# The last two whole-tile stores of a row-gradient kernel move from the SP queue to the ACT queue

## The chip, the core and the metric

The kernel runs on one core of a Trainium2 chip. The metric is the device time of one execution in microseconds (us). Five executions of the kernel before took 1249.83 to 1254.77 us, with a median of 1252.14 us. One further execution was recorded by the profiler; its own time is given with the profile below.

## The reference

The input `x` is a matrix of 8192 x 8192 float32 values, and the output has the same shape:

```python
def reference(x):
    return np.gradient(x, axis=1)
```

Along each row, every inner element is half the difference of its right and its left neighbour. The first element of a row is `x[1] - x[0]`, and the last one is `x[8191] - x[8190]`. Every value is read once and written once: 268.44 MB in and 268.44 MB out.

## The kernel before, in words

**Tiling.** The 8192 rows are cut into 32 sets (`nsets`) of 256 rows. A set lies in SBUF as one tile of 128 partitions, with `R = 2` whole rows of the matrix in each partition, so a set is 16384 float32 per partition (64 KB) and 8.39 MB in all. There are `NB = 3` tiles, called slots; set `i` uses slot `i % 3`. Each slot has 64 spare elements in front, so that the result can be written in place, shifted by those 64 elements.

**What happens to a set.** SP issues the load (line 72). GpSimd (POOL), in `put_aside` (line 84), takes the four end differences of each partition into a small tile `ends`. VectorE (DVE), in `work` (line 102), computes the half differences of the whole tile in place with one custom instruction. A small copy (line 116) puts the end values from `ends` into the result; it is done by ScalarE (ACT) for odd sets and by DVE for even ones (`placer`). Then the `storer` engine waits for that copy (line 117) and issues the store to HBM (line 118).

**The order of transfers.** There are two hardware DMA queues in use, one fed by SP and one by ACT. Each is served in the order in which its engine issued. SP's program is: loads 0, 1 and 2 at once; after that, one load per set. Before load `i` (from 3 on), SP waits at lines 68 and 69 for two things: that load `i - 1` has landed, and that the store which empties the slot, that of set `i - 3`, has landed. Below, this pair of waits is called the gate.

**The end of the program.** Sets 0 to 28 are followed by a further load, and their stores are issued by ACT. Set 31 is loaded as two halves, row 0 and row 1 of each partition (4.19 MB each, with 32 KB per partition), so that its work and its stores go row by row, all on DVE and SP. In the order of the program, SP does the following at the end:

1. load 30 (gate: load 29 and store 27);
2. the gate of load 31 (load 30 and store 28), then the two row loads of set 31;
3. the stores of sets 29 and 30 (`i + NB < nsets` is false for these two), each after a wait for its copy;
4. the stores of row 0 and row 1 of set 31, each after a wait for its copy;
5. the last waits for all stores (lines 140 and 142).

An engine's instructions run in order, so what stands behind a wait on SP is not issued before that wait is over.

Of the kernel before, what the change touches and what calls it, by code (L numbers as in the profile page):

```python
# [1 line left out]

# [4 lines left out]


@with_exitstack
def kernel(  # L10
    ctx: ExitStack,
    tc: tile.TileContext,
    x: bass.AP,
    out: bass.AP,
):

    nc = tc.nc
    P = nc.NUM_PARTITIONS
    n, m = x.shape
    R = 2
    NB = 3
    SH = 64  # L30
    W = R * m
    nsets = n // (P * R)
    f32 = x.dtype

    x_sets = x.rearrange("(s p t) m -> s p (t m)", p=P, t=R)
    out_sets = out.rearrange("(s p t) m -> s p (t m)", p=P, t=R)

    pool = ctx.enter_context(tc.tile_pool(name="pool", bufs=1))
    slots = [pool.tile([P, SH + W], f32, name=f"slot{k}", tag=f"slot{k}") for k in range(NB)]
    ends = pool.tile([P, nsets, R, 2], f32, name="ends", tag="ends")  # L40

    with tc.tile_critical():  # L42
        ld = [nc.alloc_semaphore(f"ld{k}") for k in range(NB)]
        st = [nc.alloc_semaphore(f"st{k}") for k in range(NB)]
        ld_rows = [nc.alloc_semaphore(f"ld_row{r}") for r in range(R)]
        st_rows = [nc.alloc_semaphore(f"st_row{r}") for r in range(R)]

        aside = [nc.alloc_semaphore("aside"), 0]
        halved = [nc.alloc_semaphore("halved"), 0]
        placed = {  # L50
            nc.vector: [nc.alloc_semaphore("placed_dve"), 0],
            nc.scalar: [nc.alloc_semaphore("placed_act"), 0],
        }

        def done(ins, counter):
            ins.then_inc(counter[0])
            counter[1] += 1
            return counter[0], counter[1]

        ld_n, st_n = [0] * NB, [0] * NB  # L60

        def load(i):
            k = i % NB
            if i < NB:
                parts = [(ld[k], 0, R)]
            else:

                nc.sync.wait_ge(ld[(i - 1) % NB], 16 * ld_n[(i - 1) % NB])
                nc.sync.wait_ge(st[k], 16 * st_n[k])  # L69
                parts = [(ld[k], 0, R)] if i < nsets - 1 else [(ld_rows[r], r, 1) for r in range(R)]  # L70
            for sem, r0, nr in parts:
                nc.sync.dma_start(
                    out=slots[k][:, SH + r0 * m : SH + (r0 + nr) * m],
                    in_=x_sets[i, :, r0 * m : (r0 + nr) * m],
                ).then_inc(sem, 16)
            ld_n[k] += 1

        def put_aside(i, r0, nr, sem, count):

            k = i % NB  # L80
            xin = slots[k][:, SH + r0 * m : SH + (r0 + nr) * m].rearrange("p (t m) -> p t m", m=m)
            nc.gpsimd.wait_ge(sem, count)
            return done(
                nc.gpsimd.tensor_sub(  # L84
                    out=ends[:, i, r0 : r0 + nr, :],
                    in0=xin[:, :, 1 : m : m - 2],
                    in1=xin[:, :, 0 : m - 1 : m - 2],
                ),
                aside,
            )  # L90

        def work(i, r0, nr, ready, placer, storer, sem):

            b = slots[i % NB]
            c0, c1 = r0 * m + 1, (r0 + nr) * m - 1
            mid = b[:, c0:c1]
            after = b[:, SH + c0 + 1 : SH + c1 + 1]
            before = b[:, SH + c0 - 1 : SH + c1 - 1]
            nc.vector.wait_ge(*ready)

            at = done(
                nc.vector._custom_dve(  # L102
                    dve_ops.TENSOR_TENSOR_REDUCE_SUB_MAX,
                    out=mid,
                    in0=after,
                    in1=before,
                    s0=0.0,
                    s1=0.5,
                ),
                halved,  # L110
            )
            res = b[:, r0 * m : (r0 + nr) * m].rearrange("p (t m) -> p t m", m=m)
            to, of = res[:, :, 0 : m : m - 1], ends[:, i, r0 : r0 + nr, :]
            placer.wait_ge(*at)
            copy = nc.scalar.copy if placer is nc.scalar else nc.vector.tensor_copy
            at = done(copy(out=to, in_=of), placed[placer])  # L116
            storer.wait_ge(*at)
            storer.dma_start(
                out=out_sets[i, :, r0 * m : (r0 + nr) * m],
                in_=b[:, r0 * m : (r0 + nr) * m],  # L120
            ).then_inc(sem, 16)

        for i in range(NB):
            load(i)
        for i in range(nsets):
            k = i % NB
            if i < nsets - 1:
                ready = put_aside(i, 0, R, ld[k], 16 * ld_n[k])
                placer = nc.scalar if i % 2 else nc.vector
                storer = nc.scalar if i + NB < nsets else nc.sync  # L130
                work(i, 0, R, ready, placer, storer, st[k])
                st_n[k] += 1
            else:
                for r in range(R):
                    ready = put_aside(i, r, 1, ld_rows[r], 16)
                    work(i, r, 1, ready, nc.vector, nc.sync, st_rows[r])
            if i + NB < nsets:
                load(i + NB)
        for r in range(R):
            nc.sync.wait_ge(st_rows[r], 16)  # L140
        for k in range(NB):
            nc.sync.wait_ge(st[k], 16 * st_n[k])


# [1 line left out]
_INS = ['x']  # L146
_OUTS = [((8192, 8192), 'float32')]


# [23 lines left out]
```

## Time and profile before

The profiled execution took 1253.39 us, and its span, from the first to the last instruction, is 1251.4 us; the remaining 2.0 us lie around the span.

| What | Value |
|---|---|
| median of five executions | 1252.14 us |
| profiled execution, its span | 1253.39 us, 1251.4 us |
| DVE busy | 554.2 us (44% of the span), 51 instructions |
| POOL busy | 15.1 us (1%) |
| ACT busy | 4.2 us |
| SP's DMA queue | 5328 packets, 293.60 MB, 54.7% of 16 engines |
| ACT's DMA queue | 4176 packets, 243.27 MB, 44.9% of 16 engines |
| mean transfer rate over the span | 429 GB/s |
| whole-tile DVE instruction (line 102) | 17.2 us |
| one-row DVE instruction (line 102) | 8.6 us |

How to read it: a DMA of 128 partitions is split over 16 DMA engines, and each engine takes 8 partitions. The page counts 9505 packets, of which 1056 are under 512 bytes. The 66 DMAs (33 loads, 33 stores) have 66 x 128 = 8448 data packets and 66 x 16 = 1056 small ones that count a semaphore up, which is 9504. So a data packet is one partition's contiguous run: 64 KB for a whole tile, 32 KB for a row of set 31. In the records of single DMA packets, which the trace also holds, a 64 KB packet takes 2.42 us on its engine and a 32 KB packet 1.21 us. Eight of the first are 19.3 us, which is what a whole tile costs the 16 engines.

### The profile page before, as it was taken

What the parts mean: (1) busy time and instruction counts of PE and PEld (TensorE: products, weight loads), DVE (VectorE), ACT (ScalarE), POOL (GpSimd) and SP (SyncE); (2) the same over time, 40 slices, a digit from 0 to 9 for tenths busy, and PEclk for the clock granted to TensorE, in tenths of its full rate; (3) what the DMA queues carried; (4) which work ended last, traced back from release to release, by engine and by line L of the source; (5) the groups of instructions that cost most, each with busy time, mean ns of one, the idle gap of its engine ahead of it and who ended that gap; (6) DMA issues with size and microseconds to landing.
All of it is one profiled execution on the core that took longest, in us unless ns stands there. A gap on an engine that the chain in (4) does not pass through costs nothing.

```text
span 1251.4 us, 254 instructions
## 1 busy us (share of the span) xinstructions
DVE 554.2 (44%) x51; ACT 4.2 (0%) x16; POOL 15.1 (1%) x37
## 2 busy tenths in 40 slices
DVE  2841552445533455433554335543355533555640
ACT  0000000000000000000000000000000000000000
POOL 0000000000000000000000000000000000000110
DMA  9999999999999999999999999999999999999998
GB/s 402 436 436 434 436 436 432 434 432 436 421 434 429 432 434 429 432 436 432 425 434 436 436 436 436 436 434 432 432 434 429 434 432 429 427 436 434 372 439 373
DMA packets 9505, 536.88 MB, mean 429 GB/s; under 512 B 1056, under 2 KB 1056, under 8 KB 1056
## 3 DMA queue, kind: packets, MB, share of 16 engines
q1 hardware_dynamic: 5328, 293.60, 54.7%
q10 hardware_dynamic: 4176, 243.27, 44.9%
q14 instruction: 1, 0.01, 0.0%
HBM read 268.44 MB, written 268.44 MB: 429 GB/s over the span
## 4 chain that ended last, share of the span: by engine, by line
DMA 92%; DVE 4%; issue 0%; POOL 0%; SPq 0%
DMA slot<-in_x_dram 89%; DVE slot L102 4%; DMA out_dram<-slot 3%; DVE slot L116 0%; POOL ends L84 0%; SPq L168 0%; SPq L69 0%; SPq L42 0%
## 5 line engine op out<-in xcount | busy, mean ns | idle before, releaser
L102 DVE CUSTOM_DVE_ANT_0 slot<-slot 128x16382 f32<-128x16382 f32 (+1 forms) x33 | 551.3, 16706 | 649.0 <-POOL ends L84 649.0
L84 POOL TENSOR_TENSOR ends<-slot 128x4 f32<-128x4 f32 (+1 forms) x33 | 14.9, 450 | 1179.5 <-DMA slot<-in_x_dram 1179.5
L116 ACT COPY slot<-ends 128x4 f32<-128x4 f32 x15 | 3.0, 197 | 1111.9 <-DVE slot L102 1111.9
L116 DVE COPY slot<-ends 128x4 f32<-128x4 f32 (+1 forms) x18 | 3.1, 172 | 0.6
L116 ACT ACT_TABLE_LOAD x1 | 1.3, 1283 | 41.1 <-DVE slot L116 41.1
L157 POOL MEMSET const-bfloat16-1.0<- 128x1 bf16 x1 | 0.1, 101 | 0.0
L157 POOL MEMSET const-uint8-127<- 128x1 uint8 x1 | 0.1, 101 | 0.0
L157 POOL MEMSET const-float32-0.0<- 128x1 f32 x1 | 0.1, 98 | 0.2 <-issue 0.2
L157 POOL MEMSET const-float32-1.0<- 128x1 f32 x1 | 0.1, 98 | 0.0
## 6 DMA issues: line engine op xcount, KB each, us to landing
slot<-in_x_dram SPq DMA_DIRECT2D x2, 4096.0 KB, 17.3
out_dram<-slot SPq DMA_DIRECT2D x2, 4096.0 KB, 45.3
slot<-in_x_dram SPq DMA_DIRECT2D x31, 38.6
out_dram<-slot ACTq DMA_DIRECT2D x29, 38.1
out_dram<-slot SPq DMA_DIRECT2D x2, 42.8
```

The source lines that it names most:

```text
L84: nc.gpsimd.tensor_sub(out=ends[:, i, r0 : r0 + nr, :], in0=xin[:, :, 1 : m : m - 2], in1=xin[:, :, 0 : m - 1 : m - 2],),
L102: nc.vector._custom_dve(dve_ops.TENSOR_TENSOR_REDUCE_SUB_MAX, out=mid, in0=after, in1=before, s0=0.0, s1=0.5,),
L116: at = done(copy(out=to, in_=of), placed[placer])
L157: nc = _bacc.Bacc("TRN2", target_bir_lowering=False, num_devices=1)
```

## The change

The choice of the engine that issues a whole-tile store is dropped; ACT issues them all. This concerns sets 29 and 30, whose stores were issued by SP. Set 29 is odd, so its copy is done by ACT as well; set 30 is even, so its copy is done by DVE. The two row stores of set 31 stay on SP, and so do all loads and all gates.

```diff
             if i < nsets - 1:
                 ready = put_aside(i, 0, R, ld[k], 16 * ld_n[k])
                 placer = nc.scalar if i % 2 else nc.vector
-                storer = nc.scalar if i + NB < nsets else nc.sync
-                work(i, 0, R, ready, placer, storer, st[k])
+                work(i, 0, R, ready, placer, nc.scalar, st[k])
                 st_n[k] += 1
```

## The prediction

> **What bounds the kernel now.** I read the page's engine rows first: DVE is busy for 44% of the span, POOL and ACT for about 1% together, so no compute engine is the bound. The chain of waits says the same by line:
>
> ```profile
> by line: DMA slot<-in_x_dram 88.6%; DVE slot L102 4.1%; DMA out_dram<-slot 3.3%; issue 0.1%; DVE slot L116 0.1%; POOL ends L84 0.0%; SPq L168 0.0%; SPq L69 0.0%; SPq L42 0.0%
> ```
>
> Transfers carry the span from end to end. So the question is whether the 16 DMA engines are ever without work. I cut the span into stretches (columns: stretch, length, DVE, ACT and POOL busy, clock, mean busy share of the DMA engines, GB/s):
>
> ```profile
> 46.00:1156.00 1110.00, 497.43 (x43) 2.76 (x14) 5.54 (x28) 1.00 1.00 433
> 1156.00:1172.00 16.00, 4.24 (x2) 0.20 (x1) 0.20 (x1) 1.00 0.74 307
> 1172.00:1250.00 78.00, 31.68 (x6) 0.00 (x0) 8.72 (x2) 1.00 0.98 417
> ```
>
> The reader is to see that the engines are full for 1110 us, and then there is one hole of 16 x (1 - 0.74) = 4.2 us, or by bytes 16 x (1 - 307/433) = 4.7 us. Both include packets cut at the stretch's ends. The records of single packets give it exactly: summed over the 16 engines and divided by 16, they idle 3.3 us between 1164.8 and 1170.3, and nowhere else between the first packet (2.0) and the last (1248.7 to 1249.2).
>
> The timeline of the end says why:
>
> ```profile
> 1139.49 29.80 SPq L72 DMA_DIRECT2D slot<-in_x_dram  x3
> 1157.03 0.20 ACT L116 COPY slot<-ends 128x4 f32<-128x4 f32 x1 [77.45 <-DVE slot L102]
> 1168.53 0.20 POOL L84 TENSOR_TENSOR ends<-slot 128x4 f32<-128x4 f32 x1 [28.79 <-DMA slot<-in_x_dram]
> 1169.34 34.80 SPq L118 DMA_DIRECT2D out_dram<-slot  x4
> ```
>
> Load 30 is issued at 1139.49 and has landed by 1168.46. Store 28 landed at 1156.4 (line 69's last wait ends there). From then on load 30 is the only transfer. Store 29 is ready at 1157.25, but it stands on SP behind the gate of load 31 and is issued only at 1169.34, 12.1 us late. When load 30 runs out, every queue is empty, until the row loads issued at 1168.5 bring their first packets at 1169.4 to 1170.3.
>
> **The change, part by part.** *What moves.* Two DMA issues of 0.34 us each go from SP to ACT, with their waits. ACT has nothing behind them: the copy of set 29 is its last work, and the wait for DVE's copy of set 30 holds up nobody. On SP only the row stores stood behind them. No load waits for stores 29 or 30. So the issues cost nothing themselves; what changes is when the packets enter the rings. The stores stay in the same set of bytes.
>
> *What it gains at most.* Before, an average engine's last packet ends at 1249.0. Count what it has left at 1160.9, the first packet boundary at which store 29 could appear: of load 30 two packets on 12 engines and three on 4 (2.25 on average), and 8 each for store 29, load 31, store 30 and the two row stores in 64 KB units, 34.25 in all. At 2.418 us each that is 82.8 us, to 1243.7. The difference of 5.3 us is the hole (3.3), the first row packets after it (1.9 instead of 1.2 us), and the last two row loads on each engine, which take 1.9 and 2.0 us instead of 1.2. With no idle anywhere, the slowest engine, about 1.5 us behind the mean (load 30's packets end between 1165.3 and 1167.8), ends at 1245.2; landing is seen 0.6 us later, 1245.8, where SP's last wait now ends at 1204.2 + 26.1 + 19.3 = 1249.6. The most to be had is 3.8 us.
>
> *What is late next.* Store 29 now runs beside load 30 and slows it: on a ring that both queues use, the records show the engines taking one packet of each in turn. Load 30's last two packets wait for a store packet each, so it ends near 1170.6 and lands at about 1171 (at 1175 on an engine with three left). The row loads are issued then; an engine in use takes 4 to 6 us to reach a new DMA (store 28: issued 1116.0, first packet 1119.3 to 1119.8; store 0: 40.67 and 46.9), so they join at about 1175, when half of store 29 is left.
>
> Now row loads of 32 KB packets compete with stores of 64 KB packets, which the trace before never shows: there the rows ran alone. Bounded from both sides: if the engines take turns by packet, the rows get one third of the bytes; if by bytes, half. [...]
>
> By packets: four store packets and four row packets alternate from 1175.4 to 1189.9. Set 30's work on DVE begins at 1171.3 and its store is issued at 1171 + 0.3 + 17.2 + 0.2 = 1188.7, joining at about 1194. Until then the rows run alone (3 to 4 packets). Then about 9 row packets face 8 of store 30, in turn. So when row 1 has landed, practically all of load 30, store 29, load 31 and store 30 is out: 26.25 packets of 2.418 us from 1160.9, 1224.4 on average, 1225.9 on the slowest engine, landed 1226.5.
>
> Behind that stands a chain that was covered before (row 1 had landed by 1191.6 and its store stood in a full queue):
>
> ```profile
> 1191.60 3.23 POOL L84 TENSOR_TENSOR ends<-slot 128x2 f32<-128x2 f32 x1 [5.56 <-DMA slot<-in_x_dram]
> 1194.89 8.68 DVE L102 CUSTOM_DVE_ANT_0 slot<-slot 128x8190 f32<-128x8190 f32 x1
> 1203.61 0.17 DVE L116 COPY slot<-ends 128x2 f32<-128x2 f32 x1
> ```
>
> POOL's 3.23 us is a wait for DVE; free, it takes 0.2. So row 1's store is issued 0.3 + 8.6 + 0.2 = 9.1 us after landing, at 1235.6. Meanwhile the only work is the row 0 store (ready at about 1207, queued behind row 1's load): 8 x 1.21 = 9.7 us from 1224.4 to 1234.1. The rings then run dry again. Row 1's first packets come 0.9 to 1.8 us after issue, as those of the rows did after 1168.5, at 1236.9; 9.7 us for eight, 0.5 for a slow first one, and 0.6 to landing end it at 1247.7.
>
> *The sum.* 1249.6 becomes 1247.7: 1.9 us gained of the 3.8. Span 1251.4 - 1.9 = 1249.5, the profiled execution 1253.39 - 1.9 = 1251.5. That execution lies 1.25 us above the median of the runs shown; the same 1.9 us off the median is **1250.2 us**.
>
> [...]
>
> **The rivals.**
>
> *The hole closes wholly.* If a row load gets its half by bytes, or if one or two of store 30's packets are still queued when row 1 lands (9 against 8 is narrow, and a packet is 2.4 us), row 1's chain is covered and the work alone sets the end: 3.8 us gained, 1248.3. For it: row 1 needs to land only 2 to 3 us earlier. [...]
>
> *Slower: small packets stretch beside large stores.* The last two row loads of each engine, just ahead of the first store packet, took 1.9 and 2.0 us instead of 1.2, so a row packet near a store can lose 0.7 to 0.8 us. Now all 16 row packets of an engine pass among store packets. At half that price each, 16 x 0.38 = 6 us are added ahead of row 1's landing, and the chain behind it shows all of it: 1250.2 + 6 = 1256.2. It overturns the gain from 0.12 us a packet, and is over 0.2% slower from 0.28. Against it: 64 KB loads and stores alternate at 2.42 us with no loss.
>
> *No change.* The later landing of load 30 and row 1 gives back everything: if row 1 lands 2 us later than worked out (one more engine with three packets, a slower join), the second dry spell is as costly as the first: 1252.1.
>
> **How the numbers follow.** 0.2% is 2.5 us, about what a measurement of this kernel can tell from no change. Half closed (1250.2, own range 1248.7 to 1251.7): 0.50. Wholly closed (1248.3): 0.25. Slower by stretched packets (1256.2): 0.16. No change (1252.1): 0.09. Faster by over 0.2% is below 1249.6: 0.3 of the first case, 0.85 of the second, little else: 0.37. Slower is 0.8 of the third, with a little of the last: 0.15. The rest, 0.48, is within. The range goes from 1247.4 (second case less the 1 us by which medians scatter) to 1253.4 (no change with the same scatter, the first step of the third case); about 0.15 is left out.
>
> **What would show it.** Store 29 issued on ACT at about 1157.3, and no dip in the DMA share around 1166: the first step. Row loads issued at 1171 to 1175 instead of 1168.5: the second. POOL's row 1 operation at about 1226 instead of 1191.6: arbitration by packets; at 1215 to 1219, by bytes. A dip in the DMA share between 1234 and 1237, and a chain that ends row 1, POOL, DVE, store: the second dry spell. Row packets of 1.6 us or more: the slower rival. I am wrong from the start if the dip near 1166 remains with store 29 issued early.

## The result, and the profile after

The changed kernel took 1249.49 us (median of 19 executions), the kernel before 1252.85 us (median of 37 on the same chips). The ratio is 0.9968, with a 95% interval of 0.9958 to 0.9977: 4.0 us faster (2.9 to 5.3). A few executions of several kernels, these two included, took 1322 to 1339 us; they are left out of every ratio here and below (the two medians alone differ by 3.4 us). The gain is more than the 0.2% that can be told from no change. The time lies inside the predicted range and 0.7 us below the predicted 1250.2. That nearness is partly luck: the prediction took its 1.9 us off a median of five executions, 1252.14, which lies 0.7 us under the median of 37. The gain itself is about twice the predicted one: what came is the first rival, "the hole closes wholly" (3.8 us). The chance given to "faster" was 0.37.

The profiled execution took 1250.89 us with a span of 1248.7 us, 2.5 us less than the profiled execution of before. The same three stretches as before (columns: stretch, length, DVE, ACT and POOL busy, clock, mean busy share of the DMA engines, GB/s):

```profile
46.00:1156.00 1110.00, 497.62 (x43) 2.77 (x14) 5.59 (x28) 1.00 1.00 433
1156.00:1172.00 16.00, 0.94 (x1) 0.20 (x1) 0.00 (x0) 1.00 1.02 442
1172.00:1250.00 78.00, 35.12 (x6) 0.00 (x0) 0.59 (x3) 1.00 0.91 393
```

The first row is unchanged, 433 GB/s. In the second, 0.74 has become 1.02 (a packet counts whole in the stretch in which it starts, which can carry a share over 1). The hole is gone: by the packet records no engine idles there. The third row is lower than before mainly because the transfers end earlier inside it.

Rows of the timeline of the end (a row that holds several DMA issues, x2 or x3, runs from the first issue to the end of the last):

```profile
1139.43 39.76 SPq L72 DMA_DIRECT2D slot<-in_x_dram  x3
1157.20 38.96 ACTq L118 DMA_DIRECT2D out_dram<-slot  x2
1178.13 0.20 POOL L84 TENSOR_TENSOR ends<-slot 128x4 f32<-128x4 f32 x1 [38.45 <-DMA slot<-in_x_dram]
1197.43 0.20 POOL L84 TENSOR_TENSOR ends<-slot 128x2 f32<-128x2 f32 x1 [19.10 <-DMA slot<-in_x_dram]
1206.58 26.97 SPq L118 DMA_DIRECT2D out_dram<-slot  x2
1224.06 0.20 POOL L84 TENSOR_TENSOR ends<-slot 128x2 f32<-128x2 f32 x1 [26.43 <-DMA slot<-in_x_dram]
```

Store 29 is issued by ACT at 1157.20 instead of 1169.34. Load 30 pays for that: POOL sees it land at 1178.13 instead of 1168.53, and the row loads are issued after that. Row 1 is seen by POOL at 1224.06 instead of 1191.60. Load 30, the rows of set 31 and DVE's work on them are all later, and the kernel is faster, because before the change the end waited for none of them: they had time to spare.

The end of the chain of waits (columns: start, length, what):

```profile
1178.46 45.53 DMA slot<-in_x_dram
1223.99 0.07 issue
1224.06 0.20 POOL ends L84
1224.26 0.02 issue
1224.29 8.70 DVE slot L102
1232.99 0.02 issue
1233.01 0.17 DVE slot L116
```

This is the chain that the prediction feared: row 1's load, POOL, DVE, copy, store. It is now the one that ended last, but it costs little. By the packet records the engines idle 0.4 us on average in front of row 1's store, between 1233.4 and 1234.2, against 3.3 us in the old hole. Below, such an idle time in front of row 1's store is called the dry spell.

### The profile page after: what moved, and what is told of

It is laid out like the page before. It is cut to its first block, busy times and chain, and to the rows that moved or that the text cites. A ratio compares the mean times of both kernels' runs of the same rounds, so it can differ in the third digit from the quotient of the medians.

```text
span 1248.7 us, 254 instructions
## 1 busy us (share of the span) xinstructions
DVE 554.4 (44%) x51; ACT 4.2 (0%) x16; POOL 6.8 (1%) x37
## 2 busy tenths in 40 slices
DMA packets 9504, 536.88 MB, mean 430 GB/s; under 512 B 1056, under 2 KB 1056, under 8 KB 1056
## 4 chain that ended last, share of the span: by engine, by line
DMA 96%; DVE 2%; issue 0%; POOL 0%; SPq 0%
DMA slot<-in_x_dram 93%; DMA out_dram<-slot 3%; DVE slot L102 2%; POOL ends L84 0%; DVE slot L116 0%; SPq L72 0%; SPq L167 0%; SPq L69 0%; SPq L42 0%
## 5 line engine op out<-in xcount | busy, mean ns | idle before, releaser
L84 POOL TENSOR_TENSOR ends<-slot 128x4 f32<-128x4 f32 (+1 forms) x33 | 6.6, 199 | 1217.2 <-DMA slot<-in_x_dram 1217.2
```

The lines of the kernel that those rows point to most:

```text
L84: nc.gpsimd.tensor_sub(out=ends[:, i, r0 : r0 + nr, :], in0=xin[:, :, 1 : m : m - 2], in1=xin[:, :, 0 : m - 1 : m - 2],),
```

## The experiments

Two explanations of the gain compete. **Theory A**: the gain is the filled hole. **Theory B**: the gain is that two queues share the last 80 us, where SP alone carried everything. Four kernels tell them apart; the diffs are against the kernel before unless another is named.

**Only store 29 on ACT**

```diff
-                storer = nc.scalar if i + NB < nsets else nc.sync
+                storer = nc.sync if i == nsets - 2 else nc.scalar
```

> Only store 29 goes to ACT; store 30 stays on SP behind the row loads. Theory A (the gain is the hole at 1165 to 1170, filled because store 29 no longer stands behind the gate): 3 to 5 us faster than before, as much as the full change; DMA share near 1.00 from 1156 to 1172; row 1 lands near 1204, since no ACT store competes with it, so no dry spell near 1233. Theory B (the gain is that two queues share the last 80 us, where SP alone carried everything): clearly less than the full change, 1 to 2 us.

Measured: 0.9973 (0.9962 to 0.9983), 3.4 us faster. The hole is filled:

```profile
1156.00:1172.00 16.00, 3.44 (x1) 0.20 (x1) 0.00 (x0) 1.00 1.03 446
```

Row 1 lands at 1211.1, later than expected since load 30 again landed only at 1178.5. After store 29 no store on ACT competes with the rows, and there is no dry spell. As A says, store 29 alone brings the gain, within the intervals.

**Only store 30 on ACT**

```diff
-                storer = nc.scalar if i + NB < nsets else nc.sync
+                storer = nc.sync if i == nsets - 3 else nc.scalar
```

> Only store 30 goes to ACT; store 29 stays on SP behind the gate of load 31. Theory A: the hole stays (share about 0.74 from 1156 to 1172), load 31 is issued near 1168.5, and the time is that of before within 1 us. Theory B: two queues are in use from about 1186 on, so most of the gain is there, 2 to 4 us faster.

Measured: 0.9992 (0.9982 to 1.0003), no difference. The stretch of the hole in this kernel:

```profile
1156.00:1172.00 16.00, 3.93 (x2) 0.20 (x1) 0.20 (x1) 1.00 0.78 322
1172.00:1250.00 78.00, 32.35 (x6) 0.00 (x0) 8.49 (x2) 1.00 0.99 422
```

The hole is there (0.78; 2.7 us by the packet records), and two queues from 1186.9 on bring nothing. B falls.

**All stores where they were, but load 31 does not wait for load 30** (it still waits for store 28; below, "no gate")

```diff
-                nc.sync.wait_ge(ld[(i - 1) % NB], 16 * ld_n[(i - 1) % NB])
+                if i < nsets - 1:
+                    nc.sync.wait_ge(ld[(i - 1) % NB], 16 * ld_n[(i - 1) % NB])
```

> All stores where they were before, but load 31 waits for store 28 alone and not for load 30, so the row loads are issued near 1156.5 behind load 30 on the same queue, and store 29 follows at about 1157.3. Theory A: no hole, 3 to 5 us faster than before, with ACT's queue empty for the last 90 us. Theory B: no gain, since SP alone carries everything from 1156 on.

Measured: 0.9965 (0.9954 to 0.9977), 4.4 us faster. The row loads stand behind load 30 on SP, and store 29 behind them:

```profile
1156.00:1172.00 16.00, 4.02 (x2) 0.20 (x1) 0.20 (x1) 1.00 0.94 406
```

The 0.94 is again a matter of which packets start inside the stretch: by the packet records no engine idles between 1110 us and the end. ACT's queue is empty for the last 90 us, and the gain is there all the same. It is the wait that cost, not the queue.

**Both stores on ACT, but ACT waits for load 30** (against the changed kernel)

```diff
             storer.wait_ge(*at)
+            if i == nsets - 3:
+                storer.wait_ge(ld[(nsets - 2) % NB], 16 * ld_n[(nsets - 2) % NB])
```

> Both stores on ACT as in the change, but ACT waits for load 30 to land before it issues store 29. Theory A: the hole is back, share about 0.74 from 1156 to 1172, and the time is that of before within 1 us. Theory B: two queues share the last 80 us, so the gain of the full change stays, 3 to 4 us.

Measured: 1.0099 (1.0086 to 1.0112), 12 us slower than before. Neither theory said that. The hole is back (2.3 us by the packet records), but most of the loss comes after it:

```profile
1172.00:1205.00 33.00, 15.67 (x2) 0.00 (x0) 0.00 (x0) 1.00 0.98 365
1205.00:1222.00 17.00, 8.86 (x2) 0.00 (x0) 0.20 (x1) 1.00 1.00 360
```

Engines busy all the time, at 360 GB/s instead of 433: the packets themselves are longer. From 1165 on, a 64 KB store packet on ACT's queue takes 2.92 us on average instead of 2.42, and a row load packet 1.41 instead of 1.21. In the changed kernel the same kinds of packets also pass each other in turn, at 2.42 and 1.21. With 16 store and 16 row packets on each engine, that is 16 x 0.50 + 16 x 0.20 = 11.2 us. Row 1 lands at 1243.4, and in front of its store the engines run dry for 3.3 us. This is the slower rival of the prediction, in a kernel where it was not looked for. Two readings: **theory C**, small packets beside large ones are slow in themselves, or **theory D**, the load and the store must start together, as they do here (store 29 is issued at 1170.06, the rows at 1169.99 and 1170.37), so that each engine moves the same place of both in turn.

**The changed kernel without the gate of load 31** (the edit of the third kernel above)

> The change, and load 31 no longer waits for load 30: its rows stand behind load 30 on SP and meet the second half of store 29 and all of store 30 on ACT, with the rows two or three partitions away from the stores' packets. Theory C (32 KB row packets and 64 KB store packets in turn are slow in themselves, which made the run with ACT's wait 13 us slower): row packets or the store packets beside them stretch well over 1.21 and 2.42 us, and the time is over that of the change by 3 us or more. Theory D (they are slow only when both DMAs start together, so that each engine's load and store walk the same partitions at once): no stretch, the same time as the change within 1 us.

Measured: 1.0012 (0.9994 to 1.0029). Stores take 2.47 us and row loads 1.25, so there is little stretch, and the dry spell in front of row 1's store is 1.6 us (row 1 lands at 1227.3). The 14 executions fall into two groups, six from 1250.75 to 1252.55 us and eight from 1255.99 to 1257.51. The profile is of the first group, so what costs 4 to 5 us more in the second was not seen. The time is what C expects, the packets are not, and D expected the time of the change: inconclusive.

**ACT waits for load 30, and set 31 is one load of 64 KB packets** (against the run with ACT's wait)

```diff
-                parts = [(ld[k], 0, R)] if i < nsets - 1 else [(ld_rows[r], r, 1) for r in range(R)]
+                parts = [(ld[k], 0, R)]
...
-                    ready = put_aside(i, r, 1, ld_rows[r], 16)
+                    ready = put_aside(i, r, 1, ld[k], 16 * ld_n[k])
```

> As the run with ACT's wait, but set 31 is loaded by one DMA of 64 KB packets; its work and stores still go by row. It starts with store 29 at load 30's landing. Theory C: no 32 KB packets meet the stores, so no stretch; load 31 lands after 16 packets in turn, near 1170 + 39 = 1209, no second dry spell; the time is that of before within 1.5 us. Theory D: the stretch stays (store packets near 2.9 us), and the time is 4 us or more above before.

Measured: 1258.19 and 1260.58 us, two executions, too few for an interval; the median of before was 1252.99 us. In the packet records, 64 KB packets that alternate with 64 KB packets still stretch until load 31 lands at 1218.6: its packets take 3.10 us on average and up to 4.4, the store packets beside them 2.55 and up to 3.05. No small packet is near, so small packets are not needed for the stretch. C falls.

**ACT waits for load 30, store 30 on SP** (against the run with ACT's wait)

```diff
-                work(i, 0, R, ready, placer, nc.scalar, st[k])
+                storer = nc.sync if i == nsets - 2 else nc.scalar
+                work(i, 0, R, ready, placer, storer, st[k])
```

> As the run with ACT's wait, but store 30 goes to SP behind the row loads, so only store 29 competes with them. Theories C and D alike: the stretch is there while store 29 runs beside row 0 (1171 to 1205) and gone after that, row 1 lands near 1215 instead of 1243, and the second dry spell is gone, since store 30 stands ready: 4 to 7 us slower than before. If instead it stays 13 us slower, the stretch and store 30's competition are not what made that run slow.

Measured: 1.0049 (1.0032 to 1.0066), 6.1 us slower than before. While store 29 lasts, its packets take 2.82 us and the row packets beside them 1.45. After it most row packets are back at 1.21 us; some of the last before store 30 are long (up to 2.15), as in the kernel before. Row 1 lands at 1214.3, and there is no dry spell in front of its store. The half of the loss that is gone is put down to store 30's stretch and the dry spell; no run separates the two.

**ACT waits for load 30, and the rows start a little after store 29** (against the run with ACT's wait; N is 4 with 128 columns a copy, or 24 with 96; the copies only pass time)

```diff
+                if i == nsets - 1:
+                    nc.sync.wait_ge(later, 1)
...
+            if i == nsets - 3:
+                for j in range(N):
+                    wait = nc.scalar.copy(out=scratch[:, j, :], in_=b[:, 0:128])
+                wait.then_inc(later, 1)
```

> As the run with ACT's wait, but SP issues the row loads only after four small ACT copies that follow store 29's issue, some 1 to 1.5 us later. Theory D (packets stretch when a load and a store walk the same partitions on the same engine at once): the rows stay within one packet of the store, so the stretch stays, store packets at 2.7 us or more on average, and the time is 9 us or more above before. Theory E (it is only chance, or the state of the rings after they ran dry): also stretched.

> The same with 24 small copies, some 5 to 7 us later, so that the rows begin two to three packets behind store 29. Theory D: the stretch shrinks by more than half (store packets under 2.6 us on average against 2.92), and the run is at least 6 us faster than the run with ACT's wait, though the rows start later. Theory E: the store packets stay near 2.9 us, and the run is slower than the run with ACT's wait by the delay, 5 us or more.

Measured: 1.0011 (1.0000 to 1.0022) and 1.0004 (0.9996 to 1.0012). Store packets take 2.47 us in both. The run with four copies:

```profile
1165.20 0.34 ACTq L124 DMA_DIRECT2D out_dram<-slot  x1
1165.59 0.90 ACT L130 COPY scratch<-slot 128x128 f32<-128x128 f32 x4 [11.99 <-DMA slot<-in_x_dram]
1166.57 1.64 SPq L76 DMA_DIRECT2D slot<-in_x_dram  x2
```

The rows are issued 1.4 us after the store instead of beside it, and 11 us come back. The expectation that they would stay within one packet of the store did not come true: their first packets come at 1171.6 to 1172.2, 5.0 us and more after the issue, when each engine has moved two store packets (from 1166.1 on). With 24 copies it has moved four. So the mechanism of D was not refuted here, and the packet records of all runs fit it. In the three stretched runs, the packet of the load and the packet of the store with the same number follow each other directly 238, 126 and 125 times; in the two late runs never; in the kernel before, between 46 and 1156 us, in 7 of the 4401 places where a load packet and a store packet follow each other. (The records do not name the engine; a packet is given to the one whose last packet ended as it started.)

That the common start costs is shown as far as this: started later, the same DMAs do not stretch (2.47 us a store packet against 2.92). Three things are not separated. In all three stretched runs the load was issued first, by 0.06 us, and in both late runs the store was; the same number of both packets may be the cause or only go with it; and the late runs were on another chip than the stretched ones, which were on two. Theory E, by which the late runs should have stretched too, falls. These two runs are also the answer that the run with ACT's wait was meant to give: both stores on ACT, hole of 3.0 and 3.3 us, stretch gone, a dry spell of 1.1 and 1.0 us, and the time is that of before. In the 24-copy run:

```profile
1156.00:1172.00 16.00, 4.26 (x2) 2.95 (x17) 0.20 (x1) 1.00 0.77 332
```

**Which way of filling the hole is best**

> The changed kernel once more, beside two that fill the hole in other ways. Theory A: 3 to 5 us faster than before, a dry spell of 0 to 2 us near 1233 that ends when row 1's store comes, and row 1 landing between 1215 and 1227.

> The kernel before with load 31 not waiting for load 30, once more. Theory A: 3 to 5 us faster than before, no dry spell at all; better than the change by 0 to 2 us if the change's dry spell is real, not better if what is left is only the scatter of packets in the 1100 us before.

> Load 31 does not wait for load 30, store 29 goes to ACT, store 30 stays on SP. Theory A: hole filled and row 1 never behind store 30, so no dry spell near 1233: as fast as the kernel without the gate, within 1 us. If it is 2 us or more slower, the mixing of row loads with an ACT store costs by itself, dry spell or not.

 (the edits of the third and the first kernel together)

| Kernel | Ratio to before | Row 1 landed | Dry spell before row 1's store |
|---|---|---|---|
| the change | 0.9971 (0.9959 to 0.9983) | 1226.4 | 0.4 to 0.8 us |
| no gate, stores on SP | 0.9954 (0.9939 to 0.9970) | 1186.3 | none |
| no gate, only store 29 on ACT | 0.9981 (0.9972 to 0.9990) | 1208.7 | none |

The kernel without the gate has the lowest ratio in both of its runs (5.8 us faster than before here, 4.4 in the first), but its intervals overlap those of the change (3.6 and 4.0), so it is at least as good and not shown to be better. Its rows never alternate with a store. The third kernel is about 3 us slower than the second, and their intervals do not overlap. By the mark set before it ran (2 us), the mixing of row loads with an ACT store costs by itself, without a dry spell. Its profile shows little stretch (store packets after 1165 take 2.48 us on average); the average engine ends at 1244.0 against 1242.8 in the second, but the slowest at 1247.1 against 1243.9, so in this execution most of the loss is that four engines lag. Whether that holds in the others was not seen.

## Why the prediction was right, and where its sum failed

**The hole and its cause: right.** It was the only idle time of the DMA engines (3.3 us by the packet records of before), it came from store 29 standing behind the gate, and it goes away with each of three edits (the change, store 29 alone, no gate) that have only this in common. Where it is left or put back, nothing is gained. Filling it is not enough by itself: the changed kernel without the gate of load 31 has no hole either and gains nothing (1.0012), with a dry spell of 1.6 us and a cause in its slower executions that was not seen.

**The most to be had: right but for small misreadings.** 1243.7 was given as the end of an average engine that never idles. In the profile after, 12 of the 16 engines end at 1243.8 to 1244.0, three at 1245.4, and one at 1246.8; this last one sets the end, landed 1247.1. The average engine ends at 1244.3, of which 0.4 are idle. The prediction had put the slowest at 1245.2 without a dry spell. So this profiled execution, at 2.5 us gained, is still between the two cases, while the comparison of all executions, 4.0 us, is at the 3.8 us of the case without one. Three readings of before are slightly off in the prediction: the hole begins at 1165.3 (not 1164.8), load 30's last packet ends at 1168.1 (not 1167.8), and an engine's report follows its last packet by 0.4 us (the 0.6 is counted from the average engine to the slowest one's report). None moves a sum by more than 0.3 us.

**Turns by packet: right, but assumed.** The sum took turns by packet, and no run had shown that for packets of two sizes; before, only equal packets alternate. The records of the profile after show it: one 64 KB store packet of 2.42 us, one 32 KB row packet of 1.21 us, and so on, from 1199.6 until the rows are in (1214 on 12 engines, 1220 to 1221 on four); between 1199.6 and 1214, 63 packets of each kind start. POOL's time, 1224.06, is near the 1226 named for turns by packet, but would not have shown it alone: the rows came 7 us later than worked out, and only the four late engines made row 1 land after the 1215 to 1219 named for turns by bytes.

**The chain behind row 1: right in length.** From landing (1223.99) to the issue of its store (1233.21) are 9.2 us, against 9.1 worked out, and its first packets follow 0.9 us later.

**The step that failed: "it ends near 1170.6 and lands at about 1171".** Load 30's last packet did end at about 1170.7 on 12 engines, but it landed at 1178.07. Two terms were missing. The landing is the last of 16 reports, one from each engine, which came from 1173.33 to 1178.07, and on three engines with three packets left one more pair of packets passed, 4.8 us; the prediction named this (1175) and then went on with 1171. And on each of the 16 engines one more packet of store 29 passed between load 30's last data and the report: the first engine has its data at 1170.56 and reports at 1173.33. 1170.6 + 4.8 + 2.4 = 1177.8.

What follows from it is the missing gain. The row loads joined at 1182.3 instead of 1175, when store 29 was almost out, and soon had the engines to themselves until store 30 came at 1199.6: on 12 engines 11 row packets in a row, where 3 to 4 were worked out. So 4 row packets there, and 5 or 6 on the four late engines, faced store 30's 8, not 9. On the 12 engines row 1 was in at about 1214.2, reported by 1217.3; the four late engines report at 1223.0 to 1224.0, 2.5 us before the 1226.5 worked out, with a packet or two of store 30 still to come. Meanwhile the 12 had store 30's last packets and the row 0 store to do until 1233.5, so the dry spell shrank from the predicted 2.8 us to 0.4. This is the rival's own condition, "one or two of store 30's packets are still queued when row 1 lands"; I had weighed it on an average engine, with a 9 that should have been a 4 to 6.

**The slower rival: wrong for this change.** Row load packets take 1.214 us on average in the profile after; of 256, only two take more than 1.25 us (1.29 and 1.35, on one engine, where two store packets took 2.9 and 3.1). The stretch exists, but it needed another start than the one this change gives. The price of half a stretch, 0.38 us a packet, was borrowed from the last two row packets before, whose stretch had nothing to do with alternation, since there rows and stores stood on one queue; without the gate, the same packets are followed by the same store at 1.21 us. What caused it there was not found.

## What to carry to other kernels

When transfers bound a kernel, ask not which queue is faster but whether any ready transfer stands behind a wait that is not its own: here 12 us of such a wait cost 3.3 us of idle engines, and removing the wait was worth as much as moving the store. When a moved transfer starts earlier, follow what it slows down by the slowest of the 16 engines, not by the average: 12 of them had reported load 30 by 1173.73, and the gate opened only with the last, at 1178.07. And before an early store is put beside the last loads, check that the work behind the last load is still covered: in these runs the dry spell ranged from nothing to 3.3 us with the time at which that load landed.

## What the runs showed of the hardware that was not expected

A load and a store that were issued within 0.4 us of each other, the load first, on two queues that had run dry slowed each other for as long as both lasted: 2.92 us a store packet instead of 2.42, and 12 us in all with the dry spell behind it. Rows issued 1.4 us after the store, whose first packets came two store packets later, did not (2.47 us a store packet). It was seen with 32 KB and with 64 KB load packets. Where it was seen, packets of the same number alternated, and hardly anywhere else; whether that is the cause is open.

A DMA's landing was not a fixed time after its last data. An engine's report came 0.4 us after its last packet where one queue was in use (load 30 before, last engine: 1168.10 and 1168.46), and one packet of the other queue later where two were (load 30 after, first engine: 1170.56 and 1173.33). The records show what passed in between. On that engine a store packet of 2.42 us follows load 30's last data packet, and only then, at 1172.98, comes a 4-byte packet of SP's queue; the report follows 0.35 us later. It was the same on all 16 engines of this load. The two queues of either profile hold 1056 such packets, and there are 1056 reports; paired in order of time, each report comes 0.27 to 0.46 us after its packet.
